# The down-projection of 40 activation blocks as seven half-size products, with operand sums made from saved activations

## The chip, the cores and the metric

The kernel runs on one core of a Trainium2 chip. The metric is the device time of one execution in microseconds (us). The engines are named as in the profile: PE is TensorE's matmul, PEld its weight load, DVE is VectorE, ACT is ScalarE, POOL is GpSimd, SP is SyncE, which issues most of the DMAs.

## The reference, cut to what matters

One encoder layer on 512 tokens of width 2048: two mixers (latent attention and a gated short convolution), an output projection with a residual, and a feed-forward part whose inner width is 5632. The change lies in the last line of the feed-forward part.

```python
h = rmsnorm(x, ffn_norm_g[l])
u = conv3_centred(h @ w_ffn_up[l], ffn_conv_w[l]) + ffn_conv_b[l]
g, val = u[..., :D_FF], u[..., D_FF:]
x = x + (jax.nn.silu(g) * val) @ w_ffn_down[l]
...
return rmsnorm(x, final_norm_g)
```

The 5632 inner columns are 44 blocks of 128. `silu(g) * val` is called the activation here; the kernel holds it transposed, as 44 blocks of 128 channels by 512 tokens.

## The kernel before, in words

All arithmetic is float32. A float32 matmul is made from three passes over operands that are each split into a high part (`hi`, rounded to the type that TensorE multiplies) and the rest (`lo`): hi by hi, hi by lo, lo by hi (`mm3`, L244). To split a tile, ACT casts it (`hi`) and DVE subtracts the cast from the source (`lo`); this is `split` at L231, whose records stand at L232 (ACT) and L229 (DVE). Every `tt` (a DVE tensor-by-tensor operation) has its record at L229 too.

The work is a list of items, each of which is a run of matmuls on PE with the weights it needs. `run` (L283) walks through the list. For each item it first prepares the weights of the items ahead (load a unit of 128 x 1024 from the DRAM array `wall` into a `raw` tile, then split it into `hi` and `lo`, three buffers each), then issues what earlier items left due (`posts`, a function with a lag in items), then the item's matmuls. A post with lag 0 comes right behind the item's own matmuls. The framework then sets the final order on each engine, and may put an instruction that can run before one that stands earlier in the list but is not ready. On the chip each engine's order is fixed.

The up-projection has 4 blocks that are done plainly (`up_plain`, L803) and 40 that are done with seven products of half size (`up_seven`, L920, on `seven`, L857), which take the place of eight: the weights are cut into four quarters a11, a12, a21, a22, the 512 tokens into two halves of 256, and sums of quarters are multiplied by sums of halves. Per block there are 7 items of 24 matmuls (8 k-blocks by three passes, 128 x 256 each, record L854). The operand sums on the activation side are made once (`make_operands`, L822) and kept in 56 of the 80 tiles of 128 x 512 that the pool `tp` has. The weight sums are made for each block: DVE adds two quarters into a `raw` tile s (`first`, L874), adds a22 to it (`plus`, L880) and later a12; a21 + a22 is made by a DMA of POOL that adds in flight (L877). The results collect in three PSUM banks f, g, h: product 1 goes to f, ACT copies f to h (`seed`, L898), and products 6, 5 and 3 are added onto it in h. The seven items of a block run products 1, 7, 6, 2, 5, 4, 3 in this order (L911). Two states between are copied out by ACT (`keep`, L902, records L905 and L925), since the next product adds onto the same bank: s7 (g behind product 7) and u2 (h behind product 6, which must be out before product 5 starts two items later).

Behind the two halves of a block come the convolution (`conv_up`, L788; records L485 to L487), the gate product and the split of the activation (`gated`, L796), and POOL writes the pair hi and lo to DRAM (`save`, L776, record L780).

The down-projection goes through the 44 blocks in chunks of 8, 8, 8, 8, 8 and 4. For each of the first five chunks `down` (L968) makes 16 items, one for each 128 output columns: `proj8` (L733) with 8 k-blocks by three passes, so 24 matmuls of 128 x 512 (record L242), and one post in which DVE adds the PSUM result to the residual tile `xr[n]`. The pairs hi and lo of a chunk come back from DRAM by SP (`restore`, L782, record L785) while the chunk before is computed. The last four blocks are done by `last_half` (L1002), first for tokens 0 to 255, then for 256 to 511, beside the final norm; their weights are split ahead of time into 32 tiles (`last_weights`, L992).

Of the kernel before, what the change touches and what calls it, by code (L numbers as in the profile page):

```python
# [43 lines left out]
P = 128  # L45
# [35 lines left out]
def unit_list():  # L81
# [18 lines left out]
    c = len(CHUNKS) - 2  # L100
    u += [("down", c, n) for n in range(KD)]
# [8 lines left out]
def pack_weights(w_in, w_q_b, w_kv_b, w_o, w_up, w_down):  # L110
# [12 lines left out]
    for i, u in enumerate(UNITS):  # L123
# [27 lines left out]
        elif k == "down":  # L151
            wall[i] = kblock(w_down, int(starts[u[1]]), 8, slice(u[2] * P, (u[2] + 1) * P))
# [17 lines left out]
def encoder_block(ctx: ExitStack, tc: tile.TileContext, gx, wall, vecs, rot, out):  # L170
# [625 lines left out]
    def gated(us, f):  # L796
        tt(us[1], us[0], us[1], ALU.mult)
        a = pair()
# [23 lines left out]
    def make_operands(i):  # L822

        (a,), (b,) = restore(("xr", 2 * i)), restore(("xr", 2 * i + 1))
        for k, t in ((2 * i, a), (2 * i + 1, b)):
            nc.vector.scalar_tensor_tensor(out=t, in0=t, scalar=col("ffn_g", k), in1=rx.r, op0=ALU.mult, op1=ALU.mult)
        u, v = ztile(), ztile()
# [12 lines left out]
        operands.append(got)  # L840
# [3 lines left out]
    def mark():  # L844

        for _ in range(2):
            banks.append(ptile()[:, :HT])
            mm(banks[-1], h2[0][0][:, :P], h2[0][0][:, :HT], True, True)

    def product(ps, w, q, start):  # L850
        n = len(operands)
        for k in range(n):
            for i, (a, b) in enumerate(((0, 0), (0, 1), (1, 0))):
                nc.tensor.matmul(ps, lhsT=w[a][:, k * P:(k + 1) * P], rhs=operands[k][q][b], start=start and k == 0 and i == 0,  # L854
                                 stop=k == n - 1 and i == 2, skip_group_check=True)

    def seven(index, units, posts):  # L857
# [21 lines left out]

        def plus(name):  # L880
# [5 lines left out]
        def bank_of(name, new):  # L886
            if new:
                z[name] = ptile()[:, :HT]
            return z[name]

        def pe(name, q, start):
            def f(w):
                if name == "h":
                    z["h"] = banks[bank]
                product(bank_of(name, start), w, q, start)
            return f

        def seed():  # L898
            z["h"] = banks[bank]
# [8 lines left out]
        def call(name, *args):  # L908
            return lambda: posts[name](*(z[a] for a in args))

        order = (("f", 1, True, load("a11", "a21"), first, [(1, seed)]),  # L911
                 ("g", 7, True, load("a22"), lambda: parts(raw["s"]), [(1, keep("s7", "g"))]),
                 ("h", 6, False, load("a12"), plus("a22"), [(1, keep("u2", "h"))]),
                 ("f", 2, False, load(), lambda: parts(raw["a12"]), [(1, call("c11", "f"))]),
                 ("h", 5, False, load(), lambda: parts(raw["a21"]), [(1, call("c22", "h", "s7"))]),
                 ("g", 4, False, load(), lambda: parts(raw["a22"]), [(1, call("c21", "g", "u2"))]),
                 ("h", 3, False, load(), plus("a12"), [(1, call("c12", "h"))]))
        return [Item(pe(b, q, start), posts=after, source=(before, make)) for b, q, start, before, make, after in order]

    def up_seven(f):  # L920
# [21 lines left out]
        its = seven(f, units, {"c11": c11, "c22": c22, "c21": c21, "c12": c12})  # L942
# [12 lines left out]
    for i in range(KD // 2):  # L955
        plain[(6, 7, 8, 9, 10, 14, 15, 16)[i]].posts.append((0, lambda i=i: make_operands(i)))
# [5 lines left out]
    acts = {}  # L962

    def fetch(fs):
        for f in fs:
            acts[f] = restore(("act", f))
# [6 lines left out]
    def fetch_xr(ns):  # L973
        for n in ns:
            (xr[n],) = restore(("xr", n))

    at = len(items) - 7
    items[at].posts.append((0, lambda: fetch(range(0, 2))))
    items[at + 4].posts.append((0, lambda: fetch(range(2, 6))))
    items[at + 5].posts.append((0, lambda: fetch(range(6, 8))))  # L980
    items[at + 5].posts.append((0, lambda: fetch_xr(range(4))))
    items[at + 6].posts.append((0, lambda: fetch_xr(range(4, KD))))
    for c in range(last):
        at = len(items)
        down(c)
        for f in range(CHUNKS[c + 1]):
            items[at + f].posts.append((0, lambda f=f, c=c: fetch([starts[c + 1] + f])))
# [14 lines left out]
    def last_half(half):  # L1002
        tk = slice(half * HT, (half + 1) * HT)
        rz = Rstd(Squares(HT), D, HT // P)
        scaled, sums = [], []
# [6 lines left out]
        for n in range(KD):  # L1012
            def pe(_, n=n):
                sums.append(ptile()[:, :HT])
                for k in range(4):
                    mm3(sums[n], wl[n], slice(k * P, (k + 1) * P), acts[starts[last] + k], k == 0, k == 3, tk)

            def post(n=n):
                x = xr[n][:, tk]
                tt(x, sums[n], x, ALU.add)  # L1020
# [5 lines left out]
            def scale(n=n):  # L1026
                if n % 2 == 0:
                    scaled.append(ztile().rearrange("p (n t) -> p n t", n=2))
                nc.scalar.activation(scaled[n // 2][:, n % 2, :], xr[n][:, tk], AF.Copy, scale=col("fin_g", n))

            add(pe, posts=[(1, post), (2, scale)])
            if half == 1 and n == 2:
                stats_sums(norms[0][0])
            if half == 1 and n == 5:
# [48 lines left out]
```

## Time and profile before

| what | value |
|---|---|
| median of 3 runs | 2095.57 us (2094.94 to 2096.96) |
| the profiled execution | 2095.81 us |
| its span, first to last instruction | 2094.0 us |
| mean granted TensorE clock | 0.992 of full speed |
| busy share PE, PEld, DVE, ACT, POOL | 99%, 88%, 66%, 43%, 10% |

A span is what the profiler saw between the first and the last instruction; the time of an execution has 1.81 us more around it. In the profile's tables "busy" is the time in which at least one instruction of the group ran, "mean ns of one" the mean duration, and "idle before" the time in which the engine stood still just ahead of them, with what it waited for last. A row of windows gives the stretch (from:to, us from the span's start), its length, the busy time of PE, PEld, DVE, ACT and POOL with the number of instructions in brackets, the granted TensorE clock (1.00 is 2.4 GHz, 0.50 is 1.2 GHz), the share of the 16 DMA engines' time and GB/s. A row of a timeline gives start, duration, engine, line, operation and in square brackets the idle time before it with its releaser.

### The profile page before, as it was taken

What the parts mean: (1) busy time and instruction counts of PE and PEld (TensorE: products, weight loads), DVE (VectorE), ACT (ScalarE), POOL (GpSimd) and SP (SyncE); (2) the same over time, 40 slices, a digit from 0 to 9 for tenths busy, and PEclk for the clock granted to TensorE, in tenths of its full rate; (3) what the DMA queues carried; (4) which work ended last, traced back from release to release, by engine and by line L of the source; (5) the groups of instructions that cost most, each with busy time, mean ns of one, the idle gap of its engine ahead of it and who ended that gap; (6) DMA issues with size and microseconds to landing.
All of it is one profiled execution on the core that took longest, in us unless ns stands there. A gap on an engine that the chain in (4) does not pass through costs nothing.

```text
span 2094.0 us, 30792 instructions
## 1 busy us (share of the span) xinstructions
PE 2064.5 (99%) x12530; PEld 1845.7 (88%) x12530; DVE 1374.0 (66%) x1645; ACT 900.1 (43%) x1254; POOL 200.2 (10%) x206
## 2 busy tenths in 40 slices
PE   9999999999999997999999999999999999999997
PEld 7888888888888886999999999999998888888887
DVE  7375786854556687888888888888886333333436
ACT  6253544432234444555555556555554121212224
POOL 5002322210000000011011011011010000000000
PEclk9999999999999998999999999999999999999999
DMA  7222222223434343465454554554559843233402
GB/s 264 88 86 81 76 75 83 69 91 106 144 130 149 136 151 99 153 181 145 158 181 141 163 178 139 167 168 141 176 159 342 314 171 111 91 101 131 151 1 81
DMA packets 95326, 291.65 MB, mean 139 GB/s; under 512 B 11088, under 2 KB 15312, under 8 KB 95184
## 3 DMA queue, kind: packets, MB, share of 16 engines
q1 hardware_dynamic: 81104, 241.44, 33.3%
q0 software_dynamic: 14080, 48.24, 9.2%
q8 instruction: 98, 1.61, 0.3%
q14 instruction: 44, 0.36, 0.1%
HBM read 258.18 MB, written 31.46 MB: 138 GB/s over the span
## 4 chain that ended last, share of the span: by engine, by line
PE 61%; DVE 1%; issue 0%; ACT 0%; DVEq 0%; ACTq 0%
PE ps L854 37%; PE ps L242 23%; DVE t L229 0%; DVE lo L229 0%; ACT hi L232 0%; DVE t L487 0%; ACT t L232 0%; DVE t L486 0%; DVEq L1078 0%; ACT t L347 0%; ACT t L905 0%; ACT st L369 0%; DVE st L370 0%; DVE st L372 0%; DVE st L374 0%
## 5 line engine op out<-in xcount | busy, mean ns | idle before, releaser
L242 PE MATMUL ps<-t,hi 128*128 128x512 f32 x3248 | 1010.2, 393 | 2.6 <-ACT t L237 2.0
L232 ACT CAST hi<-raw 128x1024 fp32r<-128x1024 f32 (+1 forms) x490 | 511.7, 1044 | 845.2 <-PE ps L242 517.0
L854 PE MATMUL ps<-t,hi 128*128 128x256 f32 x4480 | 791.9, 281 | 14.0 <-ACT t L905 5.0
L242 PEld LDWEIGHTS ps<-t,hi 128*128 128x128 f32 x3248 | 610.5, 188 | 140.2 <-ACT t L237 2.9
L229 DVE TENSOR_TENSOR lo<-raw,hi 128x1024 fp32r<-128x1024 f32 (+1 forms) x489 | 602.6, 1233 | 190.6 <-ACT hi L232 180.2
L854 PEld LDWEIGHTS ps<-t,hi 128*128 128x128 f32 x4480 | 682.5, 188 | 16.1 <-ACT t L905 5.2
L242 PE MATMUL ps<-t,lo 128*128 128x512 f32 x1632 | 638.5, 393 | 0.0
L854 PE MATMUL ps<-t,lo 128*128 128x256 f32 x2240 | 614.2, 280 | 0.0
L229 DVE TENSOR_TENSOR t<-ps,t 128x512 f32<-128x512 f32 (+2 forms) x337 | 198.8, 600 | 433.4 <-PE ps L242 354.6
L854 PEld LDWEIGHTS ps<-t,lo 128*128 128x128 f32 x2240 | 417.1, 189 | 0.0
L242 PEld LDWEIGHTS ps<-t,lo 128*128 128x128 f32 x1632 | 307.6, 189 | 66.4 <-issue 0.5
L229 DVE TENSOR_TENSOR t<-t 128x512 f32<-128x512 f32 (+4 forms) x276 | 185.0, 685 | 20.9 <-ACT t L341 11.7
L229 DVE TENSOR_TENSOR raw<-raw 128x1024 f32<-128x1024 f32 x120 | 146.0, 1217 | 0.0
L780 POOL DMA_DIRECT2D act<-t x88 | 60.0, 681 | 764.9 <-ACT t L232 753.6
L242 PE MATMUL ps<-t 128*128 128x256 f32 (+1 forms) x642 | 107.5, 326 | 0.0
L242 PEld LDWEIGHTS ps<-t 128*128 128x128 f32 x642 | 94.8, 189 | 10.4
L232 ACT CAST t<-t 128x512 fp32r<-128x512 f32 (+2 forms) x109 | 63.2, 601 | 42.8 <-DVE t L229 32.4
L229 POOL TENSOR_TENSOR t<-t 128x512 f32<-128x512 f32 x39 | 64.3, 1649 | 73.1 <-DVE t L229 48.5
L341 ACT ACTIVATE t<-l 128x512 f32<-128x512 f32 x44 | 27.5, 627 | 45.2 <-DVE l L229 45.0
L667 DVE RECIPROCAL t<-t 128x512 f32<-128x512 f32 x8 | 26.8, 3352 | 24.2 <-POOL t L652 24.1
L877 POOL DMA_DIRECT2D raw<-wall x40 | 35.9, 897 | 64.5 <-DVE raw L229 41.0
L486 DVE SCALAR_TENSOR_TENSOR t<-t,vec 128x511 f32<-128x511 f32 x52 | 38.6, 743 | 1.7 <-ACT t L485 0.9
(80 smaller groups left out, 736.4 us busy)
## 6 DMA issues: line engine op xcount, KB each, us to landing
raw<-wall SPq DMA_DIRECT2D x372, 512.0 KB, 3.8
act<-t POOLq DMA_DIRECT2D x88, 256.0 KB, 5.4
t<-act SPq DMA_DIRECT2D x88, 256.0 KB, 5.8
raw<-wall POOLq DMA_DIRECT2D x40, 512.0 KB, 6.9
t<-xr SPq DMA_DIRECT2D x32, 256.0 KB, 5.3
t<-gx SPq DMA_DIRECT2D x16, 256.0 KB, 3.7
xr<-l POOLq DMA_DIRECT2D x16, 256.0 KB, 2.4
out<-t SPq DMA_DIRECT2D x16, 256.0 KB, 2.6
```

The costliest lines, as they stand in the source:

```text
L229: (eng or nc.vector).tensor_tensor(out=o, in0=a, in1=b, op=op)
L232: nc.scalar.copy(out=dst[0], in_=src)
L242: nc.tensor.matmul(ps, lhsT=w, rhs=x, start=start, stop=stop)
L341: nc.scalar.activation(sq, src, AF.Square)
L486: nc.vector.scalar_tensor_tensor(out=o[:, 1:], in0=p[:, :T - 1], scalar=w[0], in1=o[:, 1:], op0=ALU.mult, op1=ALU.add)
L667: nc.vector.reciprocal(ri, pr[hd, TB])
L780: nc.gpsimd.dma_start(o, t.bitcast(F32))
L854: nc.tensor.matmul(ps, lhsT=w[a][:, k * P:(k + 1) * P], rhs=operands[k][q][b], start=start and k == 0 and i == 0, stop=k == n - 1 and i == ...
L877: nc.gpsimd.dma_start(raw["a21"], wall[UIDX[units["a22"]]], accum_op=ALU.add)
```

## The change

The chunks 0 to 4 (40 of 44 blocks) are now multiplied with the same seven-product scheme. Four output blocks n = 4m + 2e + i (e, i in 0, 1) form a group m; i picks the row of the quarters, e the half of the PSUM bank, and the k-blocks of a chunk are taken in four pairs. A group of a chunk is 7 items of 24 matmuls of 128 x 256, where it was 4 items of 24 matmuls of 128 x 512; there are 5 chunks of 4 groups. The weights are packed into as many units as before (80), in another order.

The activation is saved as one float32 tile for these 40 blocks, no longer as a pair; the split in `gated` is left out for them. `sums_of` brings two blocks back and makes the operand sums of the pair with `make_operands`. For chunk 0 the four calls hang on the last block of the up-projection, for chunk c + 1 one call hangs behind the third item of each group of chunk c (lag 0).

The residual sits in 16 tiles `xt` in another layout. The results are taken straight into it: six DVE operations of 128 x 512 per group, among them one each for s7 and u2, which ACT copies took in the up-projection. With `lean`, the weight sum for a group's last item is made by a second adding DMA of POOL (s + a12) and not by DVE.

```diff
-        if c < len(CHUNKS) - 2:
-            u += [("down", c, n) for n in range(KD)]
...
+    u += [("ds", c, m, i, j) for c in range(len(CHUNKS) - 1) for m in range(KD // 4) for i in range(2) for j in range(2)]
...
+            w = w_down[8 * P * u[1]:8 * P * (u[1] + 1)].reshape(4, 2, P, 4, 2, 2, P)[:, u[4], :, u[2], :, u[3]]
+            wall[i] = w.transpose(1, 2, 0, 3).reshape(P, UW)
...
     def gated(us, f):
         tt(us[1], us[0], us[1], ALU.mult)
+        if f < starts[last]:
+            save(("act", f), [us[1]])
+            return
         a = pair()
         split(a, us[1])
         save(("act", f), a)
...
-    def make_operands(i):
-
+    def normed_operands(i):
         (a,), (b,) = restore(("xr", 2 * i)), restore(("xr", 2 * i + 1))
...
+        operands.append(make_operands(a, b))
+
+    def make_operands(a, b):
...
+    def product(ps, w, q, start, ops):
+        n = len(ops)
+        for e in range(UW // P // n):
+            for k in range(n):
+                c = (e * n + k) * P
+                for i, (a, b) in enumerate(((0, 0), (0, 1), (1, 0))):
+                    nc.tensor.matmul(half(ps, e), lhsT=w[a][:, c:c + P], rhs=ops[k][q][b], start=start and e == k == i == 0,
+                                     stop=k == n - 1 and i == 2, skip_group_check=True)
...
+        def a12():
+            w = parts(raw["a12"])
+            if lean:
+                nc.gpsimd.dma_start(raw["s"], wall[UIDX[units["a12"]]], accum_op=ALU.add)
+            return w
...
+        kept, kept2 = [() if a in posts else (a,) for a in ("s7", "u2")]
         order = (("f", 1, True, load("a11", "a21"), first, [(1, seed)]),
...
+                 ("g", 7, True, load("a22"), lambda: parts(raw["s"]), [(1, call("s7", "g") if "s7" in posts else keep("s7", "g"))]),
+                 ("h", 6, False, load("a12"), plus("a22"), [(1, call("u2", "h") if "u2" in posts else keep("u2", "h"))]),
+                 ("f", 2, False, load(), a12, [(1, call("c11", "f"))]),
+                 ("h", 5, False, load(), lambda: parts(raw["a21"]), [(1, call("c22", "h", *kept))]),
+                 ("g", 4, False, load(), lambda: parts(raw["a22"]), [(1, call("c21", "g", *kept2))]),
+                 ("h", 3, False, load(), (lambda: parts(raw["s"])) if lean else plus("a12"), [(1, call("c12", "h"))]))
...
-    def down(c):
-        for n in range(KD):
-            proj8(("down", c, n), lambda: [acts[starts[c] + k] for k in range(8)],
-                  [(1, lambda ps, n=n: tt(xr[n], ps, xr[n], ALU.add))])
...
+    def fetch_xr(m):
+        for a in range(2):
+            for h in range(2):
+                xt[m, a, h] = ztile()
+                for e in range(2):
+                    nc.sync.dma_start(half(xt[m, a, h], e), half(saved[("xr", 4 * m + 2 * e + a)][0][0], h))
+
+    def sums_of(c, i):
+        (a,), (b,) = (restore(("act", starts[c] + 2 * i + j)) for j in range(2))
+        sums.setdefault(c, []).append(make_operands(a, b))
+
+    def down_seven(c, m):
+        def onto(a, h, op):
+            def f(ps):
+                tt(xt[m, a, h], xt[m, a, h], ps, op)
+            return f
+
+        units = {f"a{i + 1}{j + 1}": ("ds", c, m, i, j) for i in range(2) for j in range(2)}
+        posts = {"s7": onto(1, 1, ALU.subtract), "u2": onto(1, 0, ALU.subtract), "c11": onto(0, 0, ALU.add),
+                 "c22": onto(1, 1, ALU.subtract), "c21": onto(1, 0, ALU.subtract), "c12": onto(0, 1, ALU.add)}
+        return seven(m, units, posts, sums.setdefault(c, []), T, True)
 
     at = len(items) - 7
...
+    for i, j in enumerate((0, 2, 4, 5)):
+        items[at + j].posts.append((0, lambda i=i: sums_of(0, i)))
+    for m in range(KD // 4):
+        items[at + (5, 6, 6, 6)[m]].posts.append((0, lambda m=m: fetch_xr(m)))
     for c in range(last):
...
+        for m in range(KD // 4):
+            its = down_seven(c, m)
+            if c + 1 < last:
+                its[2].posts.append((0, lambda c=c, m=m: sums_of(c + 1, m)))
+            items.extend(its)
...
     for n in range(KD // 2):
-        items[-2 * (KD // 2 - n)].posts.append((0, lambda n=n: last_weights(n)))
+        items[-1 if n == KD // 2 - 1 else -15 + 2 * n].posts.append((0, lambda n=n: last_weights(n)))
```

## Rows read from the trace of the kernel before

**Rows 1.** The page's busy times of the whole span, by engine.

```profile
PE 2064.5 (99%) x12530; PEld 1845.7 (88%) x12530; DVE 1374.0 (66%) x1645; ACT 900.1 (43%) x1254; POOL 200.2 (10%) x206
```

**Rows 2.** Windows by stage: seven-product up-projection, down-projection of 40 blocks, tail.

```profile
780.60:1593.90 813.30, 799.30 (x6725) 797.24 (x6724) 667.47 (x749) 469.33 (x652) 80.26 (x121) 0.99 0.52 159
1593.90:2035.00 441.10, 441.10 (x1938) 362.28 (x1937) 164.27 (x180) 92.44 (x99) 1.09 (x2) 1.00 0.43 153
2035.00:2094.00 59.00, 47.22 (x387) 46.40 (x386) 35.84 (x87) 27.47 (x68) 0.00 (x0) 0.93 0.22 72
```

**Rows 3.** PE: a window of the up-projection; timeline, first and last down-projection matmuls.

```profile
943.00:1106.00 163.00, 163.00 (x1386) 163.00 (x1385) 135.28 (x151) 95.61 (x132) 16.05 (x24) 1.00 0.51 156
...
1593.75 0.40 PE L242 MATMUL ps<-t,lo 128*128 128x512 f32 x1
...
2032.54 0.39 PE L242 MATMUL ps<-t,lo 128*128 128x512 f32 x1
```

**Rows 4.** Groups by line and shape: busy, mean ns of one, idle before.

```profile
L229 DVE TENSOR_TENSOR lo<-raw,hi 128x1024 fp32r<-128x1024 f32 x483 | 596.6, 1236 | 188.7 <-ACT hi L232 178.3 <-PE ps L242 9.5 <-DMA t<-act 0.7
L232 ACT CAST hi<-raw 128x1024 fp32r<-128x1024 f32 x483 | 507.4, 1051 | 831.5 <-PE ps L242 506.2 <-PE ps L854 243.2 <-issue 72.2
L229 DVE TENSOR_TENSOR raw<-raw 128x1024 f32<-128x1024 f32 x120 | 146.0, 1217 | 0.0
L229 DVE TENSOR_TENSOR t<-ps,t 128x512 f32<-128x512 f32 x200 | 135.5, 688 | 359.6 <-PE ps L242 345.9 <-DMA t<-xr 4.0 <-DMA t<-act 3.4
L229 DVE TENSOR_TENSOR t<-t 128x512 fp32r<-128x512 f32 x100 | 77.5, 794 | 6.0 <-PE ps L242 3.7 <-ACT t L232 2.0
L232 ACT CAST t<-t 128x512 fp32r<-128x512 f32 x100 | 59.8, 617 | 37.4 <-DVE t L229 32.4 <-DVE t L831 5.1
L905 ACT COPY t<-ps 128x256 f32<-128x256 f32 x80 | 25.7, 372 | 0.0
L229 DVE TENSOR_TENSOR t<-t 128x256 f32<-128x256 f32 x44 | 18.0, 421 | 8.4 <-ACT t L341 8.0
L385 ACT COPY t<-ps 128x512 f32<-128x512 f32 x6 | 3.5, 588 | 11.0 <-PE ps L242 11.0
```

**Rows 5.** Timeline of DVE in the up-projection, one crowded stretch.

```profile
1399.81 1.22 DVE L229 TENSOR_TENSOR lo<-raw,hi 128x1024 fp32r<-128x1024 f32 x1
1400.95 1.22 DVE L229 TENSOR_TENSOR raw<-raw 128x1024 f32<-128x1024 f32 x1
1402.08 0.68 DVE L229 TENSOR_TENSOR t<-t 128x512 f32<-128x512 f32 x1
1402.69 1.22 DVE L229 TENSOR_TENSOR lo<-raw,hi 128x1024 fp32r<-128x1024 f32 x1
```

**Rows 6.** DMA issues: what, by which queue, how many, KB each, us to landing.

```profile
t<-act SPq DMA_DIRECT2D x88, 256.0 KB, 5.8
raw<-wall POOLq DMA_DIRECT2D x40, 512.0 KB, 6.9
```

**Rows 7.** Timeline of SP in the down-projection: activations brought back.

```profile
1678.67 6.52 SPq L785 DMA_DIRECT2D t<-act  x10
```

**Rows 8.** Windows of the last up-projection block, and of two stretches at the first.

```profile
1574.00:1593.80 19.80, 19.80 (x169) 19.71 (x168) 15.26 (x18) 11.26 (x16) 1.09 (x2) 1.00 0.73 255
...
795.00:800.00 5.00, 3.86 (x15) 3.34 (x16) 4.66 (x8) 4.32 (x7) 0.00 (x0) 0.50 0.01 3
...
810.00:815.00 5.00, 4.44 (x21) 4.44 (x22) 0.69 (x1) 1.05 (x4) 1.08 (x2) 0.50 0.49 186
```

**Rows 9.** Matmuls L854 by shape: busy, mean ns, idle before and its releasers.

```profile
L854 PE MATMUL ps<-t,hi 128*128 128x256 f32 x4480 | 791.9, 281 | 14.0 <-ACT t L905 5.0 <-ACT t L232 4.9 <-DVE t L229 3.6
```

**Rows 10.** Timeline of ACT and PE where the first up-projection blocks stall last.

```profile
809.61 0.62 ACT L232 CAST t<-t 128x512 fp32r<-128x512 f32 x1 [1.90 <-DVE t L229]
810.14 0.64 ACT L905 COPY t<-ps 128x256 f32<-128x256 f32 x2
...
810.56 0.80 PE L854 MATMUL ps<-t,hi 128*128 128x256 f32 x2 [5.00 <-ACT t L905]
```

More of the change, by code (lines that the diff above doesn't have):

```diff
@@ L839, in make_operands @@
                 got[q] = half(p[0], j), half(p[1], j)
-        operands.append(got)
+        return got
     banks = []
@@ L846, in mark, with seven @@
         for _ in range(2):
[L847 to L857, printed above, removed]
+            banks.append(ptile())
+            mm(banks[-1], h2[0][0][:, :P], h2[0][0], True, True)
+    def product(ps, w, q, start, ops):
[6 more added lines that the diff above has]
+                                     stop=k == n - 1 and i == 2, skip_group_check=True)
+    def seven(index, units, posts, ops, wide=HT, lean=False):
         z, raw = {}, {}
@@ L887, in bank_of @@
             if new:
-                z[name] = ptile()[:, :HT]
+                z[name] = ptile()[:, :wide]
             return z[name]
@@ L892, in f @@
             def f(w):
-                if name == "h":
-                    z["h"] = banks[bank]
-                product(bank_of(name, start), w, q, start)
+                product(bank_of(name, start), w, q, start, ops)
             return f
         def seed():
-            z["h"] = banks[bank]
+            z["h"] = banks[bank][:, :wide]
             nc.scalar.copy(out=z["h"], in_=z["f"])
@@ L941, in up_seven @@
         units = {f"a{s + 1}{j + 1}": ("up", s, f, j) for s in range(2) for j in range(2)}
-        its = seven(f, units, {"c11": c11, "c22": c22, "c21": c21, "c12": c12})
+        its = seven(f, units, {"c11": c11, "c22": c22, "c21": c21, "c12": c12}, operands)
         its[-1].posts.append((2, lambda: gated(us, f)))
@@ L979, in encoder_block, with part_of @@
[L979 to L982, printed above, removed]
-    for c in range(last):
[L984 to L987, printed above, removed]
+    acts, xt, sums = {}, {}, {}
+    def part_of(n, h):
+        return half(xt[n // 4, n % 2, h], n % 4 // 2)
@@ L990, in encoder_block @@
+    for i in range(4):
+        items[-25 + 2 * i].posts.append((0, lambda i=i: fetch(starts[last] + i)))
     wl = []
@@ L1013, in pe @@
             def pe(_, n=n):
-                sums.append(ptile()[:, :HT])
+                out_ps.append(ptile()[:, :HT])
                 for k in range(4):
-                    mm3(sums[n], wl[n], slice(k * P, (k + 1) * P), acts[starts[last] + k], k == 0, k == 3, tk)
+                    mm3(out_ps[n], wl[n], slice(k * P, (k + 1) * P), acts[starts[last] + k], k == 0, k == 3, tk)
             def post(n=n):
-                x = xr[n][:, tk]
-                tt(x, sums[n], x, ALU.add)
+                x = part_of(n, hf)
+                tt(x, out_ps[n], x, ALU.add)
                 if n < KD - 1:
@@ L1028, in scale @@
                     scaled.append(ztile().rearrange("p (n t) -> p n t", n=2))
-                nc.scalar.activation(scaled[n // 2][:, n % 2, :], xr[n][:, tk], AF.Copy, scale=col("fin_g", n))
+                nc.scalar.activation(scaled[n // 2][:, n % 2, :], part_of(n, hf), AF.Copy, scale=col("fin_g", n))
             add(pe, posts=[(1, post), (2, scale)])
-            if half == 1 and n == 2:
+            if hf == 1 and n == 2:
                 stats_sums(norms[0][0])
-            if half == 1 and n == 5:
+            if hf == 1 and n == 5:
                 stats_spread(norms[0][0], [(1 + i, lambda i=i, z=norms[0]: z[1](i, z[0].r)) for i in range(KD // 2)])
```

29 lines of the change are left out of this document (7 added, 22 removed).

## The prediction

> **What bounds the kernel now.** I read the page's busy times first [rows 1]: PE is at work for 99% of the span. The average hides stages, so the windows come next [rows 2]: in the down-projection PE is busy for 441.1 of 441.1 us while DVE works for 164 and ACT for 92. Nothing waits there; the stage is as long as its matmuls. The up-projection, which already has seven products, is PE-bound too apart from 14.0 us of idle at its start [rows 2, 9]. So only fewer or shorter matmuls can help the stage, as long as DVE and ACT keep up with what replaces them.
>
> **PE's part.** The 40 blocks run from 1593.75 to the last 128x512 matmul at 2032.54, which takes its turn of 0.23 us: 439.0 us for 5 x 16 x 24 = 1920 matmuls, or 0.2287 each [rows 3]. The new form has 5 x 4 x 7 x 24 = 3360 of 128x256. Their price stands in the up-projection, where the same shape comes in the same order: 163.00 us for 1386, so 0.1176 each [rows 3], or 2.82 us per item of 24. 3360 x 0.1176 = 395.1. **PE: -43.9 us.** Against a full eighth (54.9) the shortfall is that half a matmul costs 0.514 of a whole one.
> The Trainium skill, in "TensorE: Matmul & The Clock Gate", section "Back-to-back issue gap", speaks against this: sustained spacing is about 81 ns at 128 columns and 131 ns at 512, so width is cheap and narrow matmuls dear. As an estimate by that page, half-way gives some 106 ns for 256, and the stage would go from 251 to 356 us, 105 slower. The rows have 229 and 118 ns, so they don't agree, and I go by the rows.
>
> **DVE's part, per group of 7 items (PE: 19.76 us).** Full durations [rows 4]: seven `lo` x 1.236 = 8.65; two weight sums x 1.217 = 2.43 (the third goes to POOL's DMA); six results into `xt` x 0.688 = 4.13. That is 15.2. For chunks 0 to 3 one `make_operands` comes on top: five half-width operations x 0.421 and three full `lo` x 0.794 = 4.49. Sum 19.7, so by durations DVE would be full. But in a crowded stretch instructions start closer than they last: 1.14 and 1.13 us after one of 1.22, 0.61 after one of 0.68 [rows 5]. With 0.08 off for each of 23, DVE needs 17.9 of 19.76 us, 90%; chunk 4 needs 14 plus the tail's weight splits. In the up-projection DVE is busy for 135 of 163 us, 83% by durations, with PE never idle [rows 3]. The old stage had 37% [rows 2].
> What DVE must deliver in time: the split of an item can start when a `wsp` buffer comes free, three items back; cast 1.05, `lo` 1.24 [rows 4], done about 2.4 us into an item and needed two items on, so 3.3 us of lead. For the rest the order on DVE decides. Rows 5 show that it isn't the list's: the sum at 1400.95 (s + a12, for item 7) stands ahead of the `lo` of 1402.69, an earlier item's. SP issued activations of the last full chunk at 1678 [rows 7], two chunks ahead of their place. So I expect operand sums to slip into DVE's gaps ahead of time, as far as 80 tiles allow: 28 + 28 for two chunks of operands, 16 for `xt`, leaving 8 for the next pair. I put small stalls at 0.2 us per group, 4 us; the bounds are 0 (as in the up-projection) and the second rival's 44. **Steady state: +4.**
>
> **ACT, POOL, SP, DMA: nothing on the path.** ACT per group: seven casts x 1.051, the seed, now 512 wide (0.588 by the nearest copy), four operand casts at most 0.617 each: 10.4 of 19.76 us [rows 4]. The seed has 2.82 us between item 1's end and item 3's start and needs a cast plus itself, 1.6. POOL loses the 40 second saves and gains 40 adding DMAs. The new one starts behind item 3's weight sum, cast and `lo` (1.22, 1.05 and 1.24, so 3.5 us into a group), lands 6.9 us later [rows 6], at 10.4, and its split must begin by 14.5 to be in time for item 7: cover 4 us. SP brings back 48 tiles, not 88; 32 half-size pieces of the residual replace 16 loads. A group moves six units of 0.52 MB and two tiles of 0.26, 3.7 MB, 186 GB/s; the last up-projection block had 255 at a share of 0.73 without a stall [rows 8].
>
> **The up-projection.** Leaving out the activation split (ACT 0.617, DVE 0.794 [rows 4]) gains nothing where PE is bound. At its start PE waits: the last stall ends at 810.56, released by an ACT copy (L905) that stands behind the cast of a block's activation at 809.61 [rows 10]. Without it the copy runs 0.5 us sooner, and an earlier split in the same DVE-bound stretch saves about 0.6. **-1.1.** Bounds: 0 and -3.
>
> **The seam.** Four `make_operands` for chunk 0 hang on the last up-projection block and can't wait: the first down item uses all four. By the spacing they ask 4 x (5 x 0.34 + 3 x 0.71) = 15.3 us of a DVE that has 19.8 - 15.3 = 4.5 us free there [rows 8]. Less that and the 3.3 us of lead, PE stands for 7.5. Catching up in items 2 and 3 of the first group, where DVE also has the last block's convolution: about 3. The first group's u2 behind a late operand sum (second rival): 2.8. After such a stall the clock is at 0.50, 1.2 GHz, as in 795 to 800 and 810 to 815 behind idle stretches [rows 8, 10]; there 21 matmuls ran in 4.44 us where 38 fit, 2 us lost, and I count 2.7. **+16.** Bounds: 4, if most sums are made early, and 22, what the like seam at the start of the up-projection lost (813.3 - 6720 x 0.1176 - 0.5 for two other matmuls [rows 2, 3]).
>
> The tail and everything ahead of 780 us stay.
> **Sum**, against the profiled execution's 2095.81 (span 2094.0 plus 1.81; 0.24 over the median of 2095.57): 2095.8 - 43.9 + 4 - 1.1 + 16 = **2070.8**.
>
> **The rivals.**
> *DVE is the bound.* If the next instruction waits until the one before is through, a group asks 19.7 us plus 1.05 in which DVE stands for the cast between s + a22 and its `lo`: 20.75, 1.0 over PE, 16 us in 16 groups in place of my 4: 2083; with stalls that add to it some 2090. For it: 83% busy already in the up-projection. Against it: the spacing in rows 5. The Trainium skill has this rule ("VectorE: DVE Perf Modes", section "The DRAIN you can't avoid"): no operation starts before the pipe is empty. Rows 5 don't agree for operations that aren't held. Chance 0.15.
> *u2 stands behind the operand sums: slower.* u2 was an ACT copy of 0.37 us [rows 4]; now it is a DVE subtraction. In the list it comes behind `sums_of`, which hangs on the very product that makes it. If DVE keeps that order, then from item 3's start: cast 1.05, `lo` 1.14, s7 0.61, the sums 3.85, the next `lo` 1.14, u2 0.61: 8.4 us, while item 5, which adds onto the same bank, wants to start at 5.64. 2.76 us of PE, in each of 16 groups: 44 us; my sum has one of these in, so 2071 + 41 - 4 = 2108. It decides above 1.7 us per group, where the gain is gone. For it: four calls hang at just this point. Against it: rows 5 and 7. Chance 0.17, part of it half-way.
> *The adding DMA is late.* 6.9 us is a median; if a crowded queue or late `lo` adds 6, ACT stands in front of item 7's cast and PE waits 2 us per group: 40 us, 2107. For it: the cover is only 4 us. Against it: the like DMA in the up-projection holds nothing up. Chance 0.06.
> *Half a matmul doesn't cost half.* The count of products is fixed by the code; only their price could fail the change. At 0.131 us each the gain is gone. For it: a half width leaves weight loads less cover (PEld is busy all the time in rows 3). Against it: 1386 in 163 us. Chance 0.04.
>
> **How the numbers follow.** My forecast holds 0.58, spread over 2053 to 2086 by the seam's and the steady state's bounds. A measurement of this kernel tells about 0.2%, 4.2 us, from no change: faster means under 2091.4, slower over 2099.8. Faster: 0.58, plus 0.09 of the first rival and 0.01 of the second. Same: 0.05 of the first, 0.03 of the second, 0.02 of the third. Slower: 0.01, 0.13, 0.04 and 0.04. The range goes from 2053 to 2103: it leaves out some 0.04 below, and above it the full second and third rivals, about 0.15.
>
> **What would show it.** Right: 128x256 matmuls 0.118 us apart through the stage; one stall of 5 to 10 us at the seam with the clock at 0.50 behind it; DVE at 85 to 95% in chunks 0 to 3; operand sums of a chunk done before its predecessor's groups reach their third item. Wrong: idle of PE before item 5 of each group released by a DVE subtraction (second rival), by an ACT cast before item 7 (third), by `lo` everywhere (first).

## The result, and the profile after

| | before | after |
|---|---|---|
| median | 2095.27 us (2094.94 to 2096.96, 4 runs) | 2071.72 us (2071.46 to 2072.55, 4 runs) |
| span of the profiled execution | 2094.0 us | 2069.7 us |
| granted clock, mean | 0.992 | 0.991 |

The ratio is 0.9887, 95% interval 0.987 to 0.9904: 23.5 us faster. The forecast was 2070.8, in a range of 2053 to 2103. The total was met, in part by luck: two of its smaller terms were not, and they cancel.

In some of the experiments' comparisons single runs, of the kernel before too, were 1.1 to 1.4% shorter than the rest at the same granted clock; they widen those intervals, and the medians of e1_sums_behind_u2 and e11_one_early, which count one each, would be 2063.8 and 2069.9 without it.

The page's busy times after (compare [rows 1]):

```profile
PE 2023.5 (98%) x13970; PEld 1881.3 (91%) x13970; DVE 1557.1 (75%) x1905; ACT 985.5 (48%) x1374; POOL 212.6 (10%) x206
```

Windows by stage after (start and end, length, then busy time and count of PE, PEld, DVE, ACT, POOL, PE's granted clock, DMA share, GB/s): the up-projection from its start, the seam, and four stretches of the down-projection.

```profile
780.00:1562.00 782.00, 772.89 (x6515) 770.98 (x6515) 629.38 (x690) 431.45 (x596) 57.62 (x81) 0.99 0.49 143
1562.00:1645.00 83.00, 72.50 (x575) 70.98 (x574) 70.86 (x99) 41.66 (x59) 6.61 (x9) 0.94 0.77 235
1645.00:1725.00 80.00, 74.07 (x621) 72.88 (x620) 77.60 (x116) 43.78 (x61) 6.88 (x8) 1.00 0.72 188
1725.00:1805.00 80.00, 78.66 (x666) 77.98 (x665) 72.09 (x96) 39.70 (x50) 6.87 (x8) 1.00 0.68 181
1805.00:1856.00 51.00, 50.05 (x426) 49.84 (x424) 41.01 (x52) 22.68 (x28) 3.42 (x4) 1.00 0.65 187
1856.00:2010.00 154.00, 154.00 (x1309) 153.96 (x1310) 125.03 (x145) 71.00 (x87) 12.88 (x15) 1.00 0.66 175
```

How to read them: the last stretch has no idle of PE, and 154.00 / 1309 = 0.1176 us per matmul, the price that [rows 3] gave. So every other window tells what it lost: its length less its count times 0.1176. (Some records of matmuls are missing, so a loss is good to about 1 us.) The seam lost 83.00 - 575 x 0.1176 = 15.4 us. Behind it the stretches lost 7.0, 1.7, 0.9 and 0: 9.6 together. The up-projection's start gained: its idle is 782.00 - 772.89 = 9.1 us, where [rows 9] had 14.0, and the slow clock behind the missing stall is gone too. The same window of the kernel before:

```profile
780.00:1562.00 782.00, 768.00 (x6460) 765.93 (x6459) 644.19 (x723) 452.11 (x628) 77.17 (x116) 0.99 0.51 155
```

That is 6515 - 6460 = 55 matmuls more in the same time, 6.5 us. Sum: -43.9 + 15.4 + 9.6 - 6.5 = -25.4, against -24.3 between the spans.

The timeline of PE after, matmuls that PE stood idle for (in brackets the idle time and what ended it): up start, seam, and one row of four like it behind the seam (1655.36, 1676.89, 1698.56, 1720.17).

```profile
787.07 0.39 PE L864 MATMUL ps<-t,hi 128*128 128x256 f32 x1 [0.77 <-DVE t L229]
794.10 0.58 PE L864 MATMUL ps<-t,hi 128*128 128x256 f32 x1 [5.93 <-ACT t L232]
796.39 0.58 PE L864 MATMUL ps<-t,hi 128*128 128x256 f32 x1 [1.71 <-DVE t L229]
798.60 0.80 PE L864 MATMUL ps<-t,hi 128*128 128x256 f32 x2 [0.47 <-ACT ps L915]
...
1581.57 0.50 PE L864 MATMUL ps<-t,hi 128*128 128x256 f32 x2 [2.89 <-ACT t L920]
1592.10 1.58 PE L864 MATMUL ps<-t,hi 128*128 128x256 f32 x4 [5.90 <-ACT hi L232]
...
1655.36 0.51 PE L864 MATMUL ps<-t,hi 128*128 128x256 f32 x2 [1.40 <-DVE t L229]
```

Three things to see. The stall of 5.00 us at 810.56 [rows 10] is no longer there. The seam has two stalls, not one. And behind it PE waits once in each of four groups for a DVE subtraction, the u2 of that group, which is through at 1655.30:

```profile
1654.62 0.68 DVE L229 TENSOR_TENSOR t<-t,ps 128x512 f32<-128x512 f32 x1
```

ACT ahead of the first seam stall, then DVE and ACT at the second, from their timelines after:

```profile
1579.59 1.65 ACT L232 CAST t<-t 128x512 fp32r<-128x512 f32 x3
1581.15 0.36 ACT L920 COPY t<-ps 128x256 f32<-128x256 f32 x1
...
1581.30 1.89 DVE L229 TENSOR_TENSOR t<-t 128x512 fp32r<-128x512 f32 x3
1588.01 0.42 DVE L229 TENSOR_TENSOR t<-t 128x256 f32<-128x256 f32 x1 [4.82 <-DMA t<-act]
...
1587.99 0.41 ACT L232 CAST t<-t 128x256 fp32r<-128x256 f32 x1 [6.48 <-DMA t<-act]
...
1591.00 1.04 ACT L232 CAST hi<-raw 128x1024 fp32r<-128x1024 f32 x1
```

SP's issues from its timeline after, at the seam and behind it (`raw<-wall` are weights, `t<-act` activations):

```profile
1564.64 0.85 SPq L785 DMA_DIRECT2D t<-act  x2
1576.74 3.87 SPq L259 DMA_DIRECT2D raw<-wall  x2
1580.66 0.96 SPq L785 DMA_DIRECT2D t<-act  x2
...
1640.17 1.84 SPq L785 DMA_DIRECT2D t<-act  x4
1662.59 1.85 SPq L785 DMA_DIRECT2D t<-act  x4
```

The first stall ends with the copy at 1581.15, which stands on ACT behind three casts of operand sums. The second ends with the weight cast at 1591.00, which stands on ACT behind the casts of the second pair's sums, and these wait for the pair's transfer. I had forecast an overloaded DVE here. It stands idle instead, for 4.82 us, until the second pair of activations has landed; SP issued that pair only at 1580.66, because its queue stood behind a weight load that waited 11.5 us on DVE. The wait in SP's queue from 1555 to 1600 (total, times, longest):

```profile
SPq L259 <- DVE t L229: 11.8, 2, 11.5
```

SP's lower rows are steady state. Four tiles per group are two `make_operands` per group, twice what the list says. By spacing that asks 2 x 3.85 + 14.0 = 21.7 us of DVE, where PE needs 19.76 for a group; the u2 stalls are indeed 21.5 to 21.7 us apart, and DVE is busy for 77.60 of 80.00 us in that window.

So the theories for the experiments: **A**, operand sums that run ahead fill DVE between 1640 and 1725 and u2 comes late for it; against **B**, DVE is too full anyway. At the seam **D**, the restores are late; against **E**, DVE's load. And **F**, the split left out of `gated` removed the stall at 810; against **G**, the order changed by chance.

### The profile page after: what moved, and what is told of

Its sections match the earlier page's. It is cut to its first block, busy times and chain, and to the rows that moved or that the text cites. A ratio compares the mean times of both kernels' runs of the same rounds, so it can differ in the third digit from the quotient of the medians.

```text
span 2069.7 us, 34189 instructions
## 1 busy us (share of the span) xinstructions
PE 2023.5 (98%) x13970; PEld 1881.3 (91%) x13970; DVE 1557.1 (75%) x1905; ACT 985.5 (48%) x1374; POOL 212.6 (10%) x206
## 4 chain that ended last, share of the span: by engine, by line
PE 88%; DVE 6%; DMA 2%; issue 1%; ACT 0%; SPq 0%; DVEq 0%; ACTq 0%
PE ps L864 51%; PE ps L242 37%; DVE t L229 2%; DVE lo L229 2%; DMA t<-act 2%; DVE raw L229 1%; DMA t<-xr 0%; ACT hi L232 0%; DVE t L836 0%; DVE t L837 0%; DMA raw<-wall 0%; DVE t L828 0%; DVE t L486 0%; DVE t L487 0%; SPq L785 0%
## 5 line engine op out<-in xcount | busy, mean ns | idle before, releaser
L864 PE MATMUL ps<-t,hi 128*128 128x256 f32 x6720 | 1188.9, 281 | 26.2 <-DVE t L229 9.3
L864 PEld LDWEIGHTS ps<-t,hi 128*128 128x128 f32 x6720 | 1024.3, 189 | 30.8 <-DVE t L229 11.5
L864 PE MATMUL ps<-t,lo 128*128 128x256 f32 x3360 | 923.5, 280 | 1.7 <-DVE lo L229 1.7
L232 ACT CAST hi<-raw 128x1024 fp32r<-128x1024 f32 (+1 forms) x550 | 573.9, 1046 | 731.7 <-PE ps L864 264.1
L229 DVE TENSOR_TENSOR lo<-raw,hi 128x1024 fp32r<-128x1024 f32 (+1 forms) x549 | 676.1, 1233 | 214.4 <-ACT hi L232 204.3
L864 PEld LDWEIGHTS ps<-t,lo 128*128 128x128 f32 x3360 | 626.3, 189 | 2.4 <-DVE lo L229 2.3
L242 PE MATMUL ps<-t,hi 128*128 128x512 f32 x1968 | 613.8, 394 | 5.3 <-ACT t L237 4.5
L242 PEld LDWEIGHTS ps<-t,hi 128*128 128x128 f32 x1968 | 369.8, 188 | 87.6 <-ACT t L237 5.4
L242 PE MATMUL ps<-t,lo 128*128 128x512 f32 x992 | 385.9, 392 | 0.0
L229 DVE TENSOR_TENSOR t<-t 128x512 fp32r<-128x512 f32 (+4 forms) x356 | 222.6, 642 | 35.1 <-DMA t<-act 14.4
L242 PEld LDWEIGHTS ps<-t,lo 128*128 128x128 f32 x992 | 186.6, 188 | 41.9 <-issue 0.5
L229 DVE TENSOR_TENSOR t<-t,ps 128x512 f32<-128x512 f32 x128 | 86.5, 681 | 18.1 <-PE ps L864 17.1
```

Of the source, the lines that this page charges most:

```text
L229: (eng or nc.vector).tensor_tensor(out=o, in0=a, in1=b, op=op)
L232: nc.scalar.copy(out=dst[0], in_=src)
L242: nc.tensor.matmul(ps, lhsT=w, rhs=x, start=start, stop=stop)
L864: nc.tensor.matmul(half(ps, e), lhsT=w[a][:, c:c + P], rhs=ops[k][q][b], start=start and e == k == i == 0, stop=k == n - 1 and i == 2, ski ...
```

## The experiments

All but the last four start from the changed kernel (2071.7 us); these four build on two of the others. Ratios are to the kernel before, whose medians in these comparisons were 2095.2 to 2096.1.

| run | median us | ratio, 95% interval | lost at the seam, us | lost 1645 to 2010, us |
|---|---|---|---|---|
| after | 2071.7 | 0.9887 (0.987 to 0.9904) | 15.4 | 9.6 |
| e1_sums_behind_u2 | 2062.9 | 0.9881 (0.9773 to 0.999) | 14.7 | 0.9 |
| e2_copies_on_act | 2117.6 | 1.0172 (1.0078 to 1.0265) | 29.1 | 40.3 |
| e3_u2_behind_sums | 2094.2 | 1.003 (0.9984 to 1.0076) | 26.7 | 22.1 |
| e6_no_lean | 2079.5 | 0.9949 (0.9891 to 1.0007) | 14.9 | 18.0 |
| e4_seam_one_pair | 2062.7 | 0.9846 (0.9831 to 0.9861) | 9.4 | 5.5 |
| e5_seam_one_sum | 2063.9 | 0.9852 (0.9837 to 0.9866) | 10.7 | 7.5 |
| e7_gated_split | 2078.9 | 0.992 (0.9903 to 0.9936) | 15.7 | 9.8 |
| e8_early_restores | 2066.0 | 0.9862 (0.9848 to 0.9877) | 12.0 | 8.1 |
| e9_both | 2058.0 | 0.9845 (0.9778 to 0.9912) | 11.3 | 0.7 |
| e10_sums_by_operand | 2073.1 | 0.9893 (0.9856 to 0.993) | 13.6 | 9.0 |
| e11_one_early | 2068.1 | 0.9866 (0.9779 to 0.9953) | 13.1 | 6.1 |
| e12_sums_behind_copy | 2059.2 | 0.9824 (0.981 to 0.9837) | 12.4 | 0.9 |

**One operand sum per group.**

```diff
-                its[2].posts.append((0, lambda c=c, m=m: sums_of(c + 1, m)))
+                its[3].posts.append((0, lambda c=c, m=m: sums_behind(c, m)))
...
+    def sums_behind(c, m):
+        with tc.issue_after(did["u2", c, m].ins):
+            sums_of(c + 1, m)
```

> Each make_operands of a down group is held on DVE behind that group's u2 subtraction, so that every group of chunks 0 to 3 has exactly one. Theory A (operand sums that run ahead at two per group fill DVE around 1640 to 1725 us, and u2 comes late for it): the four stalls of 1.4 us released by the u2 subtraction go, the loss behind the seam falls from 10.0 to at most 3 us, and the time from 2071.7 to 2063 to 2066. Rival B (DVE's 19.7 us per group are too many for 19.76 wherever the sums stand): the loss is only spread over all sixteen groups, 8 to 16 us, and the time is 2070 to 2078.

Theory A. Two windows of this kernel, 1645 to 1725 and 1725 to 1805:

```profile
1645.00:1725.00 80.00, 78.60 (x664) 78.30 (x663) 72.79 (x99) 40.04 (x51) 6.88 (x8) 1.00 0.68 186
1725.00:1805.00 80.00, 80.00 (x684) 79.89 (x683) 69.52 (x92) 39.36 (x50) 6.89 (x8) 1.00 0.66 185
```

The loss behind the seam falls from 9.6 to 0.9, the time by 8.8. Every group has one sum now, 19.7 us by durations; DVE is busy for 69.52 of 80.00 us, and in the second window PE never stands. So B falls, and with it the first rival of the prediction. The edit does two things: it bounds the count of sums in a group, and it puts u2 ahead of the sum. That the count was at fault rests on the busy DVE (77.60 of 80.00 us) and on the spacing of the stalls, 21.5 to 21.7 us; two sums per group with u2 ahead of them were not run.

**u2 and s7 as ACT copies again.**

```diff
-        posts = {"s7": onto(1, 1, ALU.subtract), "u2": onto(1, 0, ALU.subtract), "c11": onto(0, 0, ALU.add),
+        posts = {"c11": onto(0, 0, ALU.add),
...
             def f(ps, *other):
+                for o in other:
+                    tt(xt[m, a, h], xt[m, a, h], o, op)
                 tt(xt[m, a, h], xt[m, a, h], ps, op)
```

> s7 and u2 are kept by ACT copies, as in the up-projection, and their two subtractions wait on DVE until c22 and c21: as many DVE operations, two 128x512 copies more on ACT; the operand sums again come one per group. Theory A (only the crowding of the sums was at fault): the same as with the sums held behind u2, 2063 to 2066. Rival C (u2's place on DVE costs PE something even with one sum per group): this kernel is faster than that one by 3 us or more.

Neither: it is 54.7 us slower than the kernel with one sum per group. What PE waited for between 1600 and 2040 (in total, times, longest):

```profile
PE ps L864 <- ACT hi L232: 17.0, 15, 2.1
PE ps L864 <- ACT t L920: 14.3, 15, 7.3
```

Its timeline, ACT and then PE, at one pair of stalls:

```profile
1806.61 1.05 ACT L232 CAST hi<-raw 128x1024 fp32r<-128x1024 f32 x1 [0.52 <-PE ps L864]
1807.56 0.61 ACT L232 CAST t<-t 128x512 fp32r<-128x512 f32 x1
1808.08 0.58 ACT L920 COPY t<-ps 128x512 f32<-128x512 f32 x1
...
1807.71 0.50 PE L864 MATMUL ps<-t,hi 128*128 128x256 f32 x2 [1.06 <-ACT hi L232]
1808.71 0.64 PE L864 MATMUL ps<-t,hi 128*128 128x256 f32 x2 [0.50 <-ACT t L920]
```

ACT works for less than half of the time, yet its queue holds PE up: the copy of u2 stands behind the cast of a weight, which waits for PE to free its buffer, and behind the cast of an operand sum. The same pair stands in 14 groups. Behind this one the clock falls to 0.50, 1.2 GHz (16 matmuls in the next 3.00 us). So it is part of the change that s7 and u2 moved to DVE: with copies on ACT, in the order that the scheduler then chose, it would have been slower than before.

**u2 forced behind the operand sums**, the order of the second rival.

```diff
+        with tc.issue_after(did["s7", c, m].ins):
+            sums_of(c + 1, m)
...
+                    with tc.issue_after(did["last"].ins):
+                        f(ps)
```

`did["last"]` is the last split of the sums, `f` the subtraction of u2.

> The order that the second rival of the prediction feared, forced: in each of the 16 groups with sums, s7, then the operand sums, then u2 on DVE. At the price of 2.76 us per group PE waits 44 us in items 5, and the time, which has 5.6 us of such waits in it now, goes to 2105 to 2112. If the wait is half hidden, 1.4 us per group as the kernel shows in four groups now: 2085 to 2090. If item 5 isn't held up by u2 at all: under 2075.

22.5 us slower than the changed kernel, so the whole gain is gone (ratio 1.003). That lies between the cases, 4 us above the range of the half-hidden one. PE's waits for DVE from 1562 to 2010 (total, times, longest), and two of them from its timeline:

```profile
PE ps L864 <- DVE t L229: 16.7, 16, 1.5
...
1690.53 0.50 PE L864 MATMUL ps<-t,hi 128*128 128x256 f32 x2 [1.06 <-DVE t L229]
1711.89 0.50 PE L864 MATMUL ps<-t,hi 128*128 128x256 f32 x2 [1.05 <-DVE t L229]
```

Fourteen of the 16 are like these (1.05 to 1.07), one per group from 1669 on; one of 1.47 us is at 1614.78, and one of 0.45 at 1600.46 stands in the changed kernel too (1601.20). So PE idles for 1.05 us per group, not 2.76. The stalls come 21.36 us apart where a group needs 19.76: 1.6 us lost per group, the rest in smaller gaps. In the program's order of matmuls the sixth item of such a group, which uses another bank, is now ahead of the fifth: the order of the list was not kept on PE either. PE's rows don't name the products, but the times at which DVE takes the results fit this order. As I read it, the 2.8 us of that item hide most of the delay.

**The third weight sum on DVE again.**

```diff
-        return seven(m, units, posts, sums.setdefault(c, []), T, True)
+        return seven(m, units, posts, sums.setdefault(c, []), T)
```

> The third weight sum of a group, s + a12, goes back from POOL's adding DMA to DVE: 1.22 us more on DVE in each of 20 groups, in durations 20.9 against 19.76 in chunks 0 to 3. If DVE is full only where two sums fall into one group (four groups): 4 x 1.14 there and little elsewhere, 2075 to 2079. If DVE is at its limit in all sixteen groups: 16 x 1.1 = 18 us, 2086 to 2092. If the adding DMA itself held items back: no change or a gain, 2066 to 2072.

7.8 us slower, just past the first case. The losses are not only in the four groups of two sums: the windows of above lose 8.6, 5.4, 1.1 and 2.8. So the adding DMA is worth its place. The third rival (it comes late) has nothing here: between 1600 and 2010 no wait of PE in the changed kernel is for an ACT cast.

**The seam: the same sums without the transfers, then without the sums.**

```diff
-        (a,), (b,) = (restore(("act", starts[c] + 2 * i + j)) for j in range(2))
+        if c or not i:
+            (a,), (b,) = (restore(("act", starts[c] + 2 * i + j)) for j in range(2))
+            pair0.append((a, b))
+        a, b = pair0[-1]
```

and for the second:

```diff
+        if c == 0 and i:
+            sums[0].append(sums[0][0])
+            return
```

> At the seam all four make_operands are made from the first restored pair of activations, as many sums and splits as before, but three pairs of transfers less; the activations of blocks 2 to 7 are left out of the products. Theory D (the sums stand behind restores that SP issues late: DVE idle for 4.8 us at 1583 to 1588): the 5.9 us stall goes, the seam's loss falls from 15.6 to 6 to 10 us and the time to 2062 to 2066. Theory E (the load of 15.3 us on DVE, and the tiles that come free late, set it): the loss stays at 13 to 16, the time at 2069 to 2072.

> At the seam one make_operands, whose operands serve as all four: three times 3.85 us of DVE work and three pairs of transfers less; the activations of blocks 2 to 7 are left out. Theory E (DVE's load): the loss falls from 15.6 to about 4 us, well below what the kernel with four sums of one pair has, and the time to 2058 to 2062. Theory D (only the transfers): the same as that kernel within 2 us.

Both leave blocks 2 to 7 out of the products and serve for their times alone. Without the late transfers the 5.9 us stall is gone and the time is 9.0 us lower, with all of DVE's 15.3 us of sums still there: theory D. PE in that kernel:

```profile
1581.56 0.50 PE L864 MATMUL ps<-t,hi 128*128 128x256 f32 x2 [2.89 <-ACT t L920]
...
1591.21 0.50 PE L864 MATMUL ps<-t,hi 128*128 128x256 f32 x2 [0.59 <-ACT hi L232]
```

Three sums fewer on top of that leave the time as it is (2063.9 against 2062.7), as theory D expected, but not because they cost nothing. From 1562 to 1615 the kernel with one sum loses 5.8 us, the other 9.3. From there to 1645 the kernel with one sum loses 4.6 anew, behind one stall:

```profile
1619.58 0.43 DVE L229 TENSOR_TENSOR t<-t 128x256 f32<-128x256 f32 x1 [4.16 <-DMA t<-act]
1619.92 1.22 DVE L229 TENSOR_TENSOR lo<-raw,hi 128x1024 fp32r<-128x1024 f32 x1
...
1621.20 0.58 PE L864 MATMUL ps<-t,lo 128*128 128x256 f32 x1 [3.14 <-DVE lo L229]
```

A sum of the next chunk, not due yet, waits at the head of DVE's queue for its transfer, and a weight's split stands behind it. So the sums' own work has a share in the seam too, some 3.4 us by these two kernels: part of theory E, though far from the whole. What stays, in both, is the first stall, of 2.89 us. The window behind it in the kernel with one sum:

```profile
1580.00:1585.00 5.00, 4.46 (x21) 4.46 (x22) 2.16 (x4) 1.03 (x4) 1.10 (x2) 0.50 1.04 217
```

The clock is at 0.50 (1.2 GHz), and in 4.46 us of work 21 matmuls run where 37.9 fit: another 2.0 us lost.

**The activation's split back in `gated`.**

```diff
         if f < starts[last]:
+            split(pair(), us[1])
             save(("act", f), [us[1]])
```

> The split of each block's activation is made again, as in the kernel before (ACT 0.62, DVE 0.79 us per block), into two tiles that nobody reads. Theory F (leaving this split out is what took away the 5.0 us stall at the start of the up-projection): the stall of an ACT copy behind the cast at about 810 us is back, 5 to 6 us more: 2076 to 2078. Rival G (that stall went for another reason, the order of the instructions): no change, 2071 to 2073.

Theory F. ACT and PE at the place of [rows 10]:

```profile
810.96 0.62 ACT L232 CAST t<-t 128x512 fp32r<-128x512 f32 x1 [1.90 <-DVE t L229]
811.49 0.64 ACT L921 COPY t<-ps 128x256 f32<-128x256 f32 x2
...
811.90 0.79 PE L865 MATMUL ps<-t,hi 128*128 128x256 f32 x2 [5.00 <-ACT t L921]
```

The cast, the wait of 1.90 in front of it, the copy behind it and the stall of 5.00 us are all back, and the time is 7.2 us up, a little more than the 5 to 6 expected. In the changed kernel ACT's timeline has that copy ahead of the block's silu (L794):

```profile
805.63 0.62 ACT L920 COPY t<-ps 128x256 f32<-128x256 f32 x2
806.14 0.64 ACT L794 ACTIVATE t<-t 128x512 f32<-128x512 f32 x1
```

Without the split the copy is not just 0.5 us sooner but in another place of the queue.

**Restores a block earlier, sums two items earlier** (`back` restores a pair; `at` is the last block's first item).

```diff
-    for i, j in enumerate((0, 2, 4, 5)):
+    for i, j in enumerate((-7, -5, -3, -1)):
+        items[at + j].posts.append((0, lambda i=i: back(0, i)))
+    for i, j in enumerate((-2, 0, 2, 4)):
         items[at + j].posts.append((0, lambda i=i: sums_of(0, i)))
```

> The restores of chunk 0 are asked for one block earlier, and its make_operands two items earlier; nothing is left out. Theory D (late transfers): DVE's 4.8 us of idle at the seam go and the loss falls by 5 to 9 us, 2063 to 2067. Theory E (DVE's load and the tiles that the up-projection's operands hold until its last items): 2070 to 2072, as two of the four sums still can't be made before the last block's products are done.

Theory D, with nothing left out: 5.7 us faster. DVE's 4.8 us of idle are gone. The seam gains 3.4 us, less than the 5 to 9 expected, the stretch behind it 1.5. To 1615 the gain is 7.2; behind that 3.5 are lost anew, where a sum of the next chunk waits on DVE for 3.35 us for its transfer, at 1622.76, as in the kernel with one sum. The edit moves the sums as well as the transfers, so the share of each is open.

**Both edits together, and three tries at the rest of the seam.** The first has the two diffs on `its[3]` and on `at`.

> The two edits that each gained alone, together: each down group's operand sums held on DVE behind its u2 subtraction, and chunk 0's restores one block and its sums two items earlier. If the two losses are separate (seam and steady state): the gains add up, 8.8 and 5.7 us, 2055 to 2060. If the later stretch only gives back what the seam gained: 2061 to 2064.

2058.0: the gains of 8.8 and 5.7 add up to within 0.8. By its median this is the fastest kernel of the study, 37.9 us below its runs of the kernel before. The seam still loses 11.3; its first stall is at 1579.12, 3.14 us, behind the copy of u2.

The next two make the four steps of all pairs (`early[i][s]`: product 1; 7 and 6; 2 and 3; 5 and 4) at these items; the second takes `((0, 0, 0, 0), (3, 3, 4, 4), (4, 4, 5, 5), (5, 5, 6, 6))`.

```diff
+    for s, js in enumerate(((3, 3, 3, 3), (3, 3, 4, 4), (5, 5, 5, 5), (6, 6, 6, 6))):
+        for i, j in enumerate(js):
+            items[at + j].posts.append((0, lambda i=i, s=s: early[i][s]()))
```

> On top of the kernel with both edits, chunk 0's sums are made operand by operand for all four pairs, not pair by pair, in the order in which the first down group's items use them (1, then 7 and 6, then 2 and 3, then 5 and 4), and none is asked for before the last block's u2 has been copied by ACT; 6 shares a tile with 7, and 4 with 5, so that sixteen tiles of the last block come free two items earlier. As many operations as before. If the first seam stall (2.9 us, released by the ACT copy of u2, which stands behind three casts of the first pair's sums) and the wait for all four pairs are a matter of order: the seam loses 3 to 7 us in place of 12 and the time is 2048 to 2054. If DVE's load of 15.3 us sets the seam's loss: the same as the kernel with both edits within 2 us.

> As the sums by operand, with the four splits for product 1 asked for at the start of the last block and the others spread over its items 4 to 7. If what is early helps: as that kernel or up to 3 us faster. If anything ahead of the copy of u2 brings back the first stall: 2 to 5 us slower than that kernel.

Both miss: 15.1 and 10.2 us slower than with both edits alone. In the first of them, between 1562 and 1600, PE is busy for 35.62 us in place of 32.59 and has no first stall, but the next 45 us lose more than that, and because it cuts the tiles of the up-projection's operands differently too, that stage's start loses 4 us of busy time (768.72 of 782.00, not 772.81) and 6 with the slow clock (53 matmuls fewer). The largest part lies elsewhere: by the table, 8.3 us from 1645 to 2010. The edits are mixed, so what each did stays open.

The last, on the kernel with both edits (`copies["u2"]` is ACT's copy in the last block):

```diff
-    for i, j in enumerate((-2, 0, 2, 4)):
-        items[at + j].posts.append((0, lambda i=i: sums_of(0, i)))
+    def sums_behind_copy(i):
+        with tc.issue_after(copies["u2"].ins):
+            sums_of(0, i)
...
+    items[at - 2].posts.append((0, lambda: sums_of(0, 0)))
+    for i, j in ((1, 3), (2, 3), (3, 4)):
+        items[at + j].posts.append((0, lambda i=i: sums_behind_copy(i)))
```

> On top of the kernel with both edits: the sums of pairs 2 to 4 of chunk 0 are asked for after the last block's u2 has been copied by ACT, and their casts held behind that copy. If the first seam stall (3.1 us, released by that copy) comes from the three casts of sums ahead of it on ACT: it falls to 1.5 us or less, its slow clock shrinks with it, and if nothing else gives, the time is 2053 to 2056. If the seam's loss is set by DVE's 15.3 us whatever the order: the stall only moves, three pairs now come later, and the time is 2058 to 2063.

PE's stalls at the seam in this last kernel:

```profile
1579.47 1.03 PE L864 MATMUL ps<-t,hi 128*128 128x256 f32 x4 [1.85 <-ACT t L920]
1588.05 0.69 PE L864 MATMUL ps<-t,hi 128*128 128x256 f32 x3 [0.37 <-ACT hi L232]
1589.31 0.38 PE L864 MATMUL ps<-t,lo 128*128 128x256 f32 x1 [0.57 <-DVE lo L229]
1593.79 0.58 PE L864 MATMUL ps<-t,hi 128*128 128x256 f32 x1 [2.71 <-ACT t L232]
1595.49 0.58 PE L864 MATMUL ps<-t,hi 128*128 128x256 f32 x1 [1.12 <-DVE t L229]
```

The casts ahead of the copy did cost something, since the first stall falls from 3.14 to 1.85. But PE stands another 4.8 us later, most of it for sums: the loss only moved, and 2059.2 is no gain. So some 11 us stay at the seam, and what sets them once the transfers are early is in part open: a copy's place on ACT and the sums' own work both have a share, and three orders of the sums did not beat the one of both edits.

## Why the prediction was right, point by point

The sum came within 0.9 us of the median, but of the terms of the sum only PE's was right in size and in mechanism. The steady state came out 5.6 us dearer and the up-projection 5.4 better than forecast, and that these cancel is luck. So is the seam's size, which had another cause.

- **PE, -43.9**: right. 0.1176 us per matmul in the stage, as in the up-projection.
- **DVE per group, 17.9 of 19.76**: right where a group has one sum. With one per group everywhere DVE is busy for 87% (69.52 of 80.00), within the 85 to 95% that I named, and PE does not stand. The Trainium skill's rule that no operation starts before the pipe is empty ("VectorE: DVE Perf Modes", section "The DRAIN you can't avoid") would have asked 20.75 us of a group, as the first rival had it; the trace of that kernel doesn't agree. The same section of the Trainium skill excepts an operation that is not held, which starts earlier, and that is what [rows 5] show; the prediction passed over this. The estimate by which the sums would slip ahead was right as well, but the conclusion was not: the prediction took running ahead as relief. It is a load: two sums in a group ask 21.7 us of DVE where PE needs 19.76.
- **Steady state, +4**: under-sized, 9.6. The failed step is "I put small stalls at 0.2 us per group": four groups with two sums lose 1.4 us each by u2's wait and more in small ones, while the last groups lose nothing. One edit takes 8.7 of the 9.6 away, by the table.
- **u2 behind the sums (second rival)**: the place was right, the price was too high. Forced in all 16 groups the wait is 1.05 us in 14 of them, and a group loses 1.6, not 2.76. The items change places on PE, which the prediction hadn't thought of. The run came to +22.5, 11 of it at the seam, not +41.
- **Seam, +16**: 15.4, by the wrong reason. The failed step is the one from DVE's load (15.3 us asked, 4.5 free, 3.3 of lead) to "PE stands for 7.5": DVE stood idle for 4.82 us of it. The stalls are a late transfer (5.9 us; removing it gave 9.0 us of time with the loss behind the seam counted in) and a copy late in ACT's queue (2.9 us); slow clock stands behind them, as forecast. The sums' own work has a smaller share, some 3.4 us by the kernels with one sum and four. The prediction put nothing on the restores: the time to landing stands in [rows 6], but it never asked when SP can issue them.
- **Up-projection, -1.1**: about -6.5. I had the place, a copy behind a cast [rows 10], and the failed step is "without it the copy runs 0.5 us sooner". The cast was what held the copy at the end of the queue, itself waiting 1.90 us for DVE; without it the copy stands 4.5 us earlier (810.14 to 805.63), and the 5.00 us of idle and the slow clock behind it went together.
- **ACT, POOL, SP: nothing on the path**: true of POOL. Of SP and ACT it fails at the seam.

## What to carry to other kernels

Ask of an operation that frees a PSUM bank not how long it takes but what is ahead of it in its engine's queue, and whether that waits: here one such place cost 7 us, and one pair in each group most of 55. Work that is not due yet may run ahead into one stretch and fill it; a bound on how far it runs (here: behind this group's own post) gave 8.8 us. If it waits for a transfer, it also holds what stands behind it in the queue: 3.14 us of PE in the kernel with one sum. Where one queue carries loads that wait for buffers and others that are needed at a fixed time, ask for the latter a stage earlier.

## What the runs showed of the hardware that I had not expected

A stall need not be long for the clock to fall behind it: in the kernel with the ACT copies PE stood idle for 1.06 us, ran two matmuls, stood for 0.50 and then worked at 0.50 of the clock (1.2 GHz). But the same pair of stalls stands in 14 groups of that kernel, and the clock fell behind nine of them and stayed at 1.00 (2.4 GHz) behind five. Two stretches of 4 us, behind the pairs that end at 1786.83 and 1808.71:

```profile
1786.90:1790.90 4.00, 4.00 (x34) 4.00 (x35) 2.71 (x5) 1.05 (x1) 0.00 (x0) 1.00 0.89 291
1808.80:1812.80 4.00, 4.00 (x21) 4.00 (x22) 2.00 (x4) 0.00 (x0) 0.00 (x0) 0.57 0.79 288
```

Where it fell, 13 matmuls fewer ran in the stretch, 1.5 us. Behind the four u2 stalls of 1.4 us in the changed kernel it did not fall: the window that has them shows 1.00. So the length of the stalls alone doesn't decide it, and these runs don't tell what does.
